# Twelve or fourteen combined block pairs in the down projection, with its casts and subtractions kept in program order

## The chip, the core and the metric

The kernel runs on one NeuronCore of a Trainium2 chip. The core has a matrix engine (TensorE, PE in the profile, with its weight loads shown apart as PEld), a vector engine (VectorE, DVE), a scalar engine (ScalarE, ACT), GpSimd (POOL) and SyncE (SP). In this kernel SP issues nearly all DMAs of weights and POOL issues a second, smaller stream. Matrix products accumulate in eight PSUM banks of 128 partitions by 512 float32 numbers.

The metric is the time of one execution on the device in microseconds (us), as the median of several runs. Lower is better.

## What is computed

One layer of a hybrid decoder: a combined input projection, eight heads of differential attention, four heads of chunked retention, an output projection with a residual, and then a gated MLP with a causal convolution. The last part is the one that matters here:

```python
def conv_glu(u, w_gate, w_up, conv_w, w_down):
    ...
    return (jax.nn.silu(gc) * (u @ w_up)) @ w_down
...
h = h + conv_glu(u, w_gate[l], w_up[l], conv_w[l], w_down[l])
out = rmsnorm(h, final_norm)
return out[:, CHUNK:]
```

Here D_MODEL is 2048, D_FF is 5632, and 256 positions are returned. The last product, the **down stage**, multiplies a 256 by 5632 matrix of activations by the 5632 by 2048 matrix `w_down`.

## The kernel before

**Three products for one.** All large products keep float32 accuracy with a faster reduced format. Each operand is split into a high part (a rounded copy) and a low part (the rest), and a product is a `triple` (lines 874 to 877) of three matmuls: high by high, high by low, low by high. For every weight tile of 128 partitions, ACT casts the raw float32 weights to the high part (`S.copy`, line 210), and DVE subtracts the high part from the raw weights to give the low part (line 211). This preparation of one entry is `prep(hf)`; the inner helper is `halves`. A cast and a subtraction go over 1024 columns in most cases.

**Stages.** The span runs through the input projection with attention and retention, the output projection, the gate and up projections (44 blocks `f` of 128 rows of D_FF, one gate and one up product each), and then the down stage, with nothing but small work after it.

**The down stage.** D_FF is cut in 44 blocks of 128. The output has 256 rows (two halves `m` of 128) and 2048 columns, worked in two *groups* `g` of 1024 columns (two halves `j` of 512 each). The blocks come in two kinds:

- `2*NS` blocks, here 24, are combined two by two into `NS` = 12 **pairs**. A pair is a 2 by 2 by 2 block product done with seven instead of eight products (a Strassen-Winograd scheme). It has four *parts* per group, each an entry that `prep` prepares: `d` with 1024 columns (two triples), `u` with 1024 columns (two triples), `t` with 1024 columns (two triples), `c` with 512 columns (one triple). After part `d` has been split, DVE also rewrites its 1024 raw columns in place as a difference (line 220), and part `t` is cast from that result.
- The remaining blocks, 20 before, are **plain**: `NPL` = 10 entries of two blocks for each 512-column half, called plain halves below. One has 1024 columns and four triples.

`down_order()` writes the order of entries: for each group some plain halves lead (`LEAD[g][0]`), then come the parts of all pairs with the remaining plain halves spread evenly between them, and some plain halves close the group (`LEAD[g][1]`). In the second group the last six (`HOLD`) are prepared but held back and multiplied at the very end.

**What sets the order of the work.** The program is written in order, and a scheduler at compile time fixes the order on each engine from its own estimate of when each instruction can run. An instruction wrapped in `keep` (`tc.keep_in_program_order`) stays in written order among the others so wrapped on its engine. `ahead(hf)` is called before each entry: it writes DMA loads for chunks that open up to six entries ahead and preparations up to three entries ahead. A prepared entry occupies one of four rings of high and low tiles (three `whi`/`wlo`, and `wx` for each fourth entry). Raw chunks rotate over five buffers (three `raw`, `sraw`, `act1`; the line with `turn`), so that the load of a chunk waits until the chunk five places before it has been read for the last time. A pair is one chunk and needs four DMAs, issued in this order on SP: its first half, the combined activations `sf`, the sums `td`, and `sw` for part `c` (lines 183 to 186). Plain chunks hold two plain halves, in one DMA of 1024 KB. `side` is a list of small tasks (joining the PSUM banks into the output, normalization), and `pump(n)` writes the next n of them.

**Sums for the pairs.** During the gate and up stage `stage()` has POOL load 768 KB of pair weights, `sums()` makes two DVE additions of 512 columns and has POOL write 512 KB back (`td`). There are two such sets for each pair. The activations of each pair are combined by DVE and ACT right after its second block (lines 835 to 847).

**Banks.** A group uses all eight PSUM banks: four for the direct outputs `(m, j)`, and four, named 1, 5, 6 and 7, for the combined products. `joined()` adds the latter into the output, `take(m, j)` adds a direct one.

Of the kernel before, what the change touches and what calls it, by code (L numbers as in the profile page):

```python
# [10 lines left out]
F32 = mybir.dt.float32  # L11
# [4 lines left out]
ALU = mybir.AluOpType  # L16
# [3 lines left out]
P = 128  # L20
# [20 lines left out]
NW = 512  # L41
# [3 lines left out]
LAM_INIT = 0.8 - 0.6 * math.exp(-0.3 * 0)  # L45
HK = KT // 2
HOLD = 6
NS = 12
KP = 2 * NS
NPL = (NF - KP) // 2  # L50
LEAD = [(4, 3), (2, HOLD + 2)]
PARTS = ("d", "u", "t", "c")
ROOMS = (0, 1, "2a", "2b", "3a", "3b")
FORMS = ("2a", "2b", "3a")
# [63 lines left out]
def trunk_kernel(ctx, tc, a, out):  # L118
    nc = tc.nc
    V, S, PE = nc.vector, nc.scalar, nc.tensor  # L120
# [74 lines left out]
    def prep(hf):  # L195
        c, s = entries[hf]
        held = len(entries) - 1 - hf
        if held < 2:
            hi, lo = [big.tile([P, 1024], F32R, tag=f"act{2 + held}{i}", name=f"end{held}{i}")
                      for i in "ab"]  # L200
        elif c >= nw and (hf - 2 * nw) % 4 == 3:
            wx = big.tile([P, 2 * 1024], F32R, tag="act0", name=f"wx{hf}")
            hi, lo = wx[:, :1024], wx[:, 1024:]
        else:
            hi = wp.tile([P, 1024], F32R, tag="whi", bufs=3, name=f"whi{hf}")
            lo = wp.tile([P, 1024], F32R, tag="wlo", bufs=3, name=f"wlo{hf}")

        def halves(src, b, e):
            with tc.high_priority() if 8 < hf < 16 else nullcontext():
                S.copy(out=hi[:, b:e], in_=src)  # L210
                V.tensor_tensor(out=lo[:, b:e], in0=src, in1=hi[:, b:e].bitcast(F32),  # L211
                                op=ALU.subtract)

        if c in mixed:
            g, p = divmod(mixed[c], NS)
            if s == "d":
                halves(raw[c][:, :2 * NW], 0, 2 * NW)
                two = raw[c][:, :2 * NW].rearrange("p (a c) -> p a c", a=2)
                t2 = raw[c][:, 2 * NW:3 * NW].unsqueeze(1).to_broadcast([P, 2, NW])
                V.tensor_tensor(out=two, in0=two, in1=t2, op=ALU.subtract)  # L220
            elif s == "u":
                halves(raw[c][:, 2 * NW:], 0, 2 * NW)
            elif s == "t":
                halves(raw[c][:, :2 * NW], 0, 2 * NW)
            else:
                halves(pools["sw"][g, p], 0, NW)
        else:
            halves(raw[c][:, s * 1024:(s + 1) * 1024], 0, 1024)
        pairs[hf] = (hi, lo)
        if s in (1, PARTS[-1]):  # L230
            raw.pop(c)
# [47 lines left out]
    def misc(name):  # L279
        return ps1.tile([P, 512], F32, tag="misc", bufs=3, name=name)  # L280
# [132 lines left out]
    def pump(n):  # L413
        for _ in range(n):
            if side:
                side.pop(0)()
# [351 lines left out]
    with ExitStack() as p2:  # L768
# [27 lines left out]
            stage()  # L796

        for f in range(NF):
            if f in (1, 2):
                stage()  # L800
            if staged and (f >= KP or f >= 4 and f % 2 == 0):
                sums()
            if f in (39, 41):
                m = (f - 39) // 2
                halfs.append(big.tile([P, D], F32, tag=f"htok{m}", name=f"htok{m}"))
                keep(nc.sync.dma_start(out=halfs[m], in_=hd[m * P:(m + 1) * P]))
            ps = gemm_q(idx, gs, 0)
            g = fw.tile([P, NQ], F32, tag="g", name=f"fg{f}")
            V.tensor_tensor(out=g, in0=ps[:, :NQ], in1=rstd2, op=ALU.mult)
            c = fw.tile([P, SEQ], F32, tag="c", name=f"fc{f}")  # L810
            V.tensor_scalar(out=c, in0=g[:, 0:SEQ], scalar1=cw[:, f, 0:1], scalar2=None,
                            op0=ALU.mult)
            for i in (1, 2):
                V.scalar_tensor_tensor(out=c, in0=g[:, i:i + SEQ], scalar=cw[:, f, i:i + 1],
                                       in1=c, op0=ALU.mult, op1=ALU.add)
            s = fw.tile([P, SEQ], F32, tag="s", name=f"fs{f}")
            S.activation(out=s, in_=c, func=AF.Silu)
            V.tensor_tensor(out=s, in0=s, in1=rstd2[:, 2:], op=ALU.mult)
            ps = gemm_t(idx + 1, gs)
            ul = fw.tile([P, SEQ], F32, tag="ul", name=f"ful{f}")  # L820
            S.copy(out=ul, in_=ps[:, SEQ:])
            u = ul
            V.tensor_tensor(out=u, in0=ps[:, :SEQ], in1=ul, op=ALU.add)
            V.tensor_tensor(out=u, in0=u, in1=s, op=ALU.mult)
            n = P if f < KP and f % 2 == 0 else SEQ
            S.copy(out=fhi[:, f, :n], in_=u[:, :n])
            V.tensor_tensor(out=flo[:, f, :n], in0=u[:, :n], in1=fhi[:, f, :n].bitcast(F32),
                            op=ALU.subtract)
            if f < KP and f % 2 == 0:
                us[f] = u  # L830
            elif f < KP:
                a1, a2 = us.pop(f - 1), u
                p = f // 2
                sm = fw.tile([P, 4, P], F32, tag="sm", bufs=1, name=f"sm{p}")
                V.tensor_tensor(out=sm[:, 0], in0=a1[:, P:], in1=a2[:, P:], op=ALU.add)
                V.tensor_tensor(out=sm[:, 1], in0=sm[:, 0], in1=a1[:, :P], op=ALU.subtract)
                V.tensor_tensor(out=sm[:, 2], in0=a1[:, :P], in1=a1[:, P:], op=ALU.subtract)
                V.tensor_tensor(out=sm[:, 3], in0=a2[:, :P], in1=sm[:, 1], op=ALU.subtract)
                s1 = fhi[:, f - 1, P:]
                S.copy(out=s1, in_=sm[:, 0])  # L840
                V.tensor_tensor(out=flo[:, f - 1, P:], in0=sm[:, 0], in1=s1.bitcast(F32),
                                op=ALU.subtract)
                sh = fw.tile([P, 2, 3, P], F32R, tag="sh", bufs=1, name=f"sh{p}")
                S.copy(out=sh[:, 0], in_=sm[:, 1:])
                V.tensor_tensor(out=sh[:, 1], in0=sm[:, 1:], in1=sh[:, 0].bitcast(F32),
                                op=ALU.subtract)
                keep(nc.gpsimd.dma_start(out=sd[p], in_=sh.rearrange("p a b c -> p (a b c)")
                                         .bitcast(F32)))
            idx += 2
# [79 lines left out]

        e = 2 * idx  # L930
        for g in range(2):
            mm = [ps1.tile([P, NW], F32, tag="mm", bufs=3, name=f"o{g}_{i}") for i in range(3)]
            bank = {(0, 0): mm[0], (0, 1): mm[1], (1, 0): mm[2], (1, 1): misc(f"o{g}_3")}
            bank[1], bank[6] = misc(f"x{g}_1"), misc(f"x{g}_6")
            xx = ps1.tile([P, 2, 512], F32, tag="sc", bufs=1, name=f"x{g}_57")
            bank[5], bank[7] = xx[:, 0], xx[:, 1]
            res = {(m, j): htok[:, m, (2 * g + j) * NW:(2 * g + j + 1) * NW]
                   for m in range(2) for j in range(2)}
            left = {1: NS, 5: NS, 6: NS, 7: NS}
# [2 lines left out]
                    left[m, j] = 2 * NPL + (NS if (m, j) != (1, 1) else 0)  # L942
            if g:
                left[1, 1] -= 2 * HOLD
            fresh = set(bank)

            def product(key, ac, wt, c0):
                left[key] -= 1
                ws = slice(c0, c0 + NW)
                triple(bank[key], *ac, wt[0][:, ws], wt[1][:, ws], key in fresh, left[key] == 0)  # L950
                fresh.discard(key)

            def joined():
                t = dn.tile([P, NW], F32, tag="t", name=f"t{g}")

                def f1():
# [23 lines left out]
            def weighed(m, n):  # L980
                return lambda: weigh(m, n * NW, (n + 1) * NW)

            def take(m, j):
                def f():
                    add(res[m, j], bank[m, j])
                return f
# [4 lines left out]
            for i, (kind, x, y) in enumerate(seq):  # L991
                ahead(e)
                if g and i >= len(seq) - HOLD:
                    held.append((y, e))
                    e += 1
                    continue
                wt = pairs[e]
                if kind == "w":
# [16 lines left out]
                if i == last_s:  # L1015
                    if g:
                        side.extend([weighed(m, n) for n in range(2) for m in range(2)])
                        side.append(lambda: norm(1))
                    side.extend(joined())
                    side.extend([take(0, 0), take(1, 0)])  # L1020
                    if g:
                        side.append(lambda: norm_scale(1))
                        for m in range(2):
                            side.extend([squared(m, 2), weighed(m, 2)])
                        side.append(lambda: S.activation(out=root, in_=so[:, 1, 2:3],
                                                         func=AF.Sqrt))
                pump(3 if i > last_s else 1)
            pump(len(side))
            if not g:
                take(0, 1)()  # L1030
                take(1, 1)()
                side.extend([nop] * 6)
                for m, n in ((0, 0), (1, 0), (0, 1), (1, 1)):
                    side.extend([squared(m, n), nop, nop])
                continue
            po = [bank[0, 1], bank[1, 1]]
            nb = NPL

# [19 lines left out]
            for c in range(2):  # L1058
# [2 lines left out]
                    down(o, 1, b, hf, c * HW, HW, start=i == 0, stop=i == HOLD - 1)  # L1061
                b_, e_ = LB + c * HW, LB + (c + 1) * HW
                hc = htok[:, 1, b_:e_]
                V.tensor_tensor(out=hc, in0=o, in1=hc, op=ALU.add)
                square(1, b_, e_, NB - 1 + c)
                weigh(1, b_, e_)
                if c == 0:
# [91 lines left out]
```

## Time and profile before

| | |
|---|---|
| median of 3 runs | 1150.26 us (1149.74 to 1150.60) |
| the profiled execution, its own time | 1150.52 us |
| its span from the first to the last instruction | 1148.4 us |
| PE busy | 1137.6 us (99% of the span) |
| DVE busy | 931.8 us (81%) |
| ACT busy | 605.7 us (53%) |
| mean granted TensorE clock | 0.999 of full speed |

The profiled execution's own time is 2.1 us longer than its span; that part lies before the first and after the last instruction. It is 0.26 us above the median of the runs. Busy time of PE overlaps with itself, since matmuls are pipelined, so 99% says that PE had work all the time, and the distance between the starts of two matmuls says how fast it went.

### The profile page before, as it was taken

What the parts mean: (1) busy time and instruction counts of PE and PEld (TensorE: products, weight loads), DVE (VectorE), ACT (ScalarE), POOL (GpSimd) and SP (SyncE); (2) the same over time, 40 slices, a digit from 0 to 9 for tenths busy, and PEclk for the clock granted to TensorE, in tenths of its full rate; (3) what the DMA queues carried; (4) which work ended last, traced back from release to release, by engine and by line L of the source; (5) the groups of instructions that cost most, each with busy time, mean ns of one, the idle gap of its engine ahead of it and who ended that gap; (6) DMA issues with size and microseconds to landing.
All of it is one profiled execution on the core that took longest, in us unless ns stands there. A gap on an engine that the chain in (4) does not pass through costs nothing.

```text
span 1148.4 us, 20659 instructions
## 1 busy us (share of the span) xinstructions
PE 1137.6 (99%) x7967; PEld 1066.1 (93%) x7967; DVE 931.8 (81%) x1738; ACT 605.7 (53%) x997; POOL 36.4 (3%) x84
## 2 busy tenths in 40 slices
PE   8999999999999999999999999999999999999997
PEld 7999999999999999999999999999999988888886
DVE  7898787667677769888888888888877778898897
ACT  7676665443345545444445444444444456556663
POOL 0000000000000000000000000100000000000000
PEclk9999999999999999999999999999999999999999
DMA  9644546565648775766776777888876588877872
GB/s 314 215 156 160 183 140 196 166 224 165 208 157 251 236 230 190 286 244 256 280 255 246 275 286 267 297 310 303 318 261 223 196 335 302 291 285 247 312 279 92
DMA packets 96018, 276.76 MB, mean 241 GB/s; under 512 B 43856, under 2 KB 52176, under 8 KB 74160
## 3 DMA queue, kind: packets, MB, share of 16 engines
q1 hardware_dynamic: 87616, 238.08, 59.7%
q0 software_dynamic: 8160, 37.23, 8.6%
q8 instruction: 62, 1.02, 0.3%
q14 instruction: 36, 0.29, 0.1%
q10 hardware_dynamic: 144, 0.14, 0.1%
HBM read 251.56 MB, written 23.86 MB: 240 GB/s over the span
## 4 chain that ended last, share of the span: by engine, by line
PE 98%; ACT 1%; DMA 0%; DVE 0%; SPq 0%; issue 0%; DVEq 0%; ACTq 0%
PE mm L463 14%; PE mm L452 10%; PE mm L450 10%; PE mm L451 10%; PE mm L442 7%; PE mm L443 7%; PE mm L444 7%; PE mm L465 7%; PE o L876 4%; PE o L877 4%; PE o L875 4%; PE x L875 2%; PE x L877 2%; PE x L876 2%; PE po L587 1%; PE ro L642 1%
## 5 line engine op out<-in xcount | busy, mean ns | idle before, releaser
L210 ACT CAST whi<-raw 128x1024 fp32r<-128x1024 f32 x379 | 397.9, 1052 | 376.6 <-issue 92.1
L211 DVE TENSOR_TENSOR wlo<-raw,whi 128x1024 fp32r<-128x1024 f32 x379 | 462.6, 1223 | 132.5 <-ACT whi L210 125.6
L463 PE MATMUL mm<-g,whi 128*128 128x512 f32 x352 | 124.4, 392 | 0.0
L452 PE MATMUL mm<-g,wlo 128*128 128x258 f32 x352 | 99.4, 282 | 0.0
L442 PE MATMUL mm<-x,whi 128*128 128x272 f32 (+1 forms) x344 | 99.3, 289 | 0.0
L450 PE MATMUL mm<-g,whi 128*128 128x260 f32 x352 | 99.2, 282 | 0.0
L444 PE MATMUL mm<-x,wlo 128*128 128x272 f32 (+1 forms) x344 | 99.0, 288 | 0.0
L443 PE MATMUL mm<-x,whi 128*128 128x272 f32 (+1 forms) x344 | 98.9, 287 | 0.0
L465 PE MATMUL mm<-g,wlo 128*128 128x256 f32 x352 | 98.6, 280 | 0.0
L451 PE MATMUL mm<-g,whi 128*128 128x256 f32 x352 | 97.8, 278 | 0.0
L463 PEld LDWEIGHTS mm<-g,whi 128*128 128x128 f32 x352 | 66.1, 188 | 13.1
L450 PE MATMUL mm<-ys,whi 128*128 128x260 f32 x256 | 71.9, 282 | 0.0
L452 PE MATMUL mm<-ys,wlo 128*128 128x258 f32 x256 | 71.8, 281 | 0.0
L451 PE MATMUL mm<-ys,whi 128*128 128x256 f32 x256 | 70.7, 276 | 0.0
L451 PEld LDWEIGHTS mm<-g,whi 128*128 128x128 f32 x352 | 66.7, 189 | 1.9
L465 PEld LDWEIGHTS mm<-g,wlo 128*128 128x128 f32 x352 | 66.2, 188 | 0.0
L450 PEld LDWEIGHTS mm<-g,whi 128*128 128x128 f32 x352 | 66.1, 188 | 0.0
L452 PEld LDWEIGHTS mm<-g,wlo 128*128 128x128 f32 x352 | 66.0, 188 | 0.0
L443 PEld LDWEIGHTS mm<-x,whi 128*128 128x128 f32 x344 | 64.9, 189 | 0.0
L444 PEld LDWEIGHTS mm<-x,wlo 128*128 128x128 f32 x344 | 64.8, 188 | 0.0
L442 PEld LDWEIGHTS mm<-x,whi 128*128 128x128 f32 x344 | 64.8, 188 | 0.0
L876 PE MATMUL o<-wlo,fhi 128*128 128x512 f32 x149 | 58.1, 390 | 0.0
(404 smaller groups left out, 3061.6 us busy)
## 6 DMA issues: line engine op xcount, KB each, us to landing
raw<-in_w_in_dram SPq DMA_DIRECT2D x44, 1024.0 KB, 4.9
raw<-in_w_gate_dram SPq DMA_DIRECT2D x44, 1024.0 KB, 5.2
raw<-in_w_up_dram SPq DMA_DIRECT2D x44, 1024.0 KB, 5.3
raw<-in_w_down_dram SPq DMA_DIRECT2D x20, 1024.0 KB, 6.7
ts<-in_w_mix_dram POOLq DMA_DIRECT2D x24, 768.0 KB, 5.1
raw<-in_w_out_dram SPq DMA_DIRECT2D x16, 1024.0 KB, 5.2
td<-ts POOLq DMA_DIRECT2D x24, 512.0 KB, 5.3
raw<-in_w_mix_dram SPq DMA_DIRECT2D x24, 512.0 KB, 6.5
```

The lines of the kernel that those rows point to most:

```text
L210: S.copy(out=hi[:, b:e], in_=src)
L211: V.tensor_tensor(out=lo[:, b:e], in0=src, in1=hi[:, b:e].bitcast(F32), op=ALU.subtract)
L442: PE.matmul(ps[:, :n], wh, xh, start=(k == 0), stop=False)
L443: PE.matmul(ps[:, :n], wh, xl, start=False, stop=False)
L444: PE.matmul(ps[:, :n], wl, xh, start=False, stop=(k == KT - 1))
L450: PE.matmul(ps[:, :NQ + 2], wh, src.cols(k, GO - 2, GL), start=(k == 0), stop=False)
L451: PE.matmul(ps[:, 4:NQ + 2], wh, src.cols(k, GL, GW), start=False, stop=False)
L452: PE.matmul(ps[:, 2:NQ + 2], wl, src.hi(k), start=False, stop=(k == KT - 1))
L463: PE.matmul(ps, wh, src.cols(k, GO + 2, GW), start=(k == 0), stop=(k == KT - 1))
L465: PE.matmul(ps[:, :SEQ], wl, src.cols(k, GO + 2, GL), start=False, stop=False)
L875: PE.matmul(o, ah, wh, start=start, stop=False)
L876: PE.matmul(o, ah, wl, start=False, stop=False)
```

## The change

Pairs go from 12 to 14, so that 28 of the 44 blocks are combined and 16 are plain (eight plain halves for each 512-column half). The lead and tail of the two groups become 4 and 6, and 4 and 8. From the fifth entry of the down stage on, casts, subtractions and the in-place difference are wrapped in `keep`. The sums in the gate and up stage run in three of four blocks from the third block on. PSUM tiles of the down stage are allocated at their first use. At the end of the first group the joining tasks are pumped one per plain half instead of three, the last two additions move into the second group, and in the second group two tasks are pumped for each held half.

```diff
-NS = 12
+NS = 14
-LEAD = [(4, 3), (2, HOLD + 2)]
+LEAD = [(4, 6), (4, HOLD + 2)]
...
+        pin = keep if hf >= 2 * nw + 4 else (lambda ins: ins)
+
         def halves(src, b, e):
             with tc.high_priority() if 8 < hf < 16 else nullcontext():
-                S.copy(out=hi[:, b:e], in_=src)
-                V.tensor_tensor(out=lo[:, b:e], in0=src, in1=hi[:, b:e].bitcast(F32),
-                                op=ALU.subtract)
+                pin(S.copy(out=hi[:, b:e], in_=src))
+                pin(V.tensor_tensor(out=lo[:, b:e], in0=src, in1=hi[:, b:e].bitcast(F32),
+                                    op=ALU.subtract))
...
-                V.tensor_tensor(out=two, in0=two, in1=t2, op=ALU.subtract)
+                pin(V.tensor_tensor(out=two, in0=two, in1=t2, op=ALU.subtract))
...
-            if f in (1, 2):
+            if f < 2:
                 stage()
-            if staged and (f >= KP or f >= 4 and f % 2 == 0):
+            elif staged and f % 4 != 3:
                 sums()
-            if f in (39, 41):
-                m = (f - 39) // 2
+            if f in (41, 42):
+                m = f - 41
...
-            mm = [ps1.tile([P, NW], F32, tag="mm", bufs=3, name=f"o{g}_{i}") for i in range(3)]
-            bank = {(0, 0): mm[0], (0, 1): mm[1], (1, 0): mm[2], (1, 1): misc(f"o{g}_3")}
-            bank[1], bank[6] = misc(f"x{g}_1"), misc(f"x{g}_6")
...
+            def room(key):
+                if key in bank:
+                    return bank[key]
+                if key in (5, 7):
+                    xx = ps1.tile([P, 2, 512], F32, tag="sc", bufs=1, name=f"x{g}_57")
+                    bank[5], bank[7] = xx[:, 0], xx[:, 1]
+                elif key in ((0, 0), (1, 0), (0, 1)):
+                    bank[key] = ps1.tile([P, NW], F32, tag="mm", bufs=3,
+                                         name=f"o{g}_{key[0]}{key[1]}")
+                else:
+                    bank[key] = misc(f"o{g}_11" if key == (1, 1) else f"x{g}_{key}")
+                return bank[key]
...
                 if g and i >= len(seq) - HOLD:
                     held.append((y, e))
                     e += 1
+                    pump(2)
                     continue
...
-                    side.extend(joined())
-                    side.extend([take(0, 0), take(1, 0)])
+                    side.extend([take(0, 0), take(1, 0), *joined()])
...
-                pump(3 if i > last_s else 1)
-            pump(len(side))
+                pump(3 if g and i > last_s else 1)
             if not g:
-                take(0, 1)()
-                take(1, 1)()
-                side.extend([nop] * 6)
+                side.extend([take(0, 1), take(1, 1)] + [nop] * 6)
...
                 continue
+            pump(len(side))
...
-                V.tensor_tensor(out=hc, in0=o, in1=hc, op=ALU.add)
+                keep(V.tensor_tensor(out=hc, in0=o, in1=hc, op=ALU.add))
```

More of the change, by code (lines that the diff above doesn't have):

```diff
@@ L931, in trunk_kernel @@
         for g in range(2):
-            mm = [ps1.tile([P, NW], F32, tag="mm", bufs=3, name=f"o{g}_{i}") for i in range(3)]
-            bank = {(0, 0): mm[0], (0, 1): mm[1], (1, 0): mm[2], (1, 1): misc(f"o{g}_3")}
-            bank[1], bank[6] = misc(f"x{g}_1"), misc(f"x{g}_6")
-            xx = ps1.tile([P, 2, 512], F32, tag="sc", bufs=1, name=f"x{g}_57")
-            bank[5], bank[7] = xx[:, 0], xx[:, 1]
+            bank = {}
+            def room(key):
[10 more added lines that the diff above has]
+                return bank[key]
             res = {(m, j): htok[:, m, (2 * g + j) * NW:(2 * g + j + 1) * NW]
@@ L944, in trunk_kernel @@
                 left[1, 1] -= 2 * HOLD
-            fresh = set(bank)
+            fresh = set(left)
             def product(key, ac, wt, c0):
@@ L949, in product, with joined @@
                 ws = slice(c0, c0 + NW)
-                triple(bank[key], *ac, wt[0][:, ws], wt[1][:, ws], key in fresh, left[key] == 0)
+                triple(room(key), *ac, wt[0][:, ws], wt[1][:, ws], key in fresh, left[key] == 0)
                 fresh.discard(key)
-            def joined():
+            def joined(bank=bank, res=res):
                 t = dn.tile([P, NW], F32, tag="t", name=f"t{g}")
@@ L981, in weighed, with take @@
                 return lambda: weigh(m, n * NW, (n + 1) * NW)
-            def take(m, j):
+            def take(m, j, bank=bank, res=res):
                 def f():
```

## The prediction

> **What bounds the kernel now.** I read the page's span and its chain first, then the busy table by stretches, then the waits of PE's weight loads.
>
> ```profile
> span 1148.4 us, 20659 instructions
> PE 98%; ACT 1%; DMA 0%; DVE 0%; SPq 0%; issue 0%; DVEq 0%; ACTq 0%
> ```
> ```profile
> core 0: us, PE busy (x) PEld busy (x) DVE busy (x) ACT busy (x) POOL busy (x), PEclk, DMA share, GB/s
> 457.00:707.00 250.00, 250.00 (x1786) 235.09 (x1785) 207.12 (x379) 122.26 (x202) 18.52 (x35) 1.00 0.71 265
> 707.00:860.00 153.00, 153.00 (x1087) 143.53 (x1086) 127.19 (x203) 69.60 (x109) 13.14 (x25) 1.00 0.83 301
> 916.00:1030.00 114.00, 114.00 (x506) 94.42 (x505) 97.76 (x99) 67.77 (x76) 0.54 (x1) 1.00 0.87 314
> 1030.00:1115.00 85.00, 85.00 (x376) 70.19 (x375) 75.35 (x71) 54.73 (x63) 0.00 (x0) 1.00 0.76 271
> 1115.00:1136.00 21.00, 21.00 (x110) 17.97 (x109) 20.96 (x30) 10.49 (x14) 0.54 (x1) 1.00 0.21 76
> ```
> ```profile
> PEld x L875 <- ACT wx L210: 0.3, 1, 0.3
> ```
>
> 98% of the chain is PE. The first two rows are gate and up, the next two the groups of the down stage, the last its tail. PE is never idle in them, at clock 1.00. The last fence is all that PE's weight loads waited from 457 us on: once, 0.3 us. So the time is the number of matmuls times their spacing. But DVE is already busy 75.35 of 85 us in the second group and 20.96 of 21 in the tail.
>
> **What goes.** A group now has 12x7 + 20x4 = 164 triples, afterwards 14x7 + 16x4 = 162. Two groups, three matmuls each: 12 matmuls of 512 columns less.
>
> ```profile
> 1050.17 0.39 PE L876 MATMUL o<-wlo,fhi 128*128 128x512 f32 x1
> ...
> 1052.89 0.39 PE L875 MATMUL o<-whi,fhi 128*128 128x512 f32 x1
> ```
>
> From the first to the last of these 13 matmuls there are 12 steps and 2.72 us, 0.227 us each. The gain is thus 12 x 0.227 = **2.72 us**; I find nothing that could make it larger.
>
> **What comes, in the down stage.** A group has four entries more (72 for 68). Two more pairs bring six 1024-column and two 512-column preparations and two in-place differences; four plain halves take four preparations away. Over both groups DVE gets 4 subtractions of 1024 columns, 4 of 512 and 4 differences.
>
> ```profile
> 1080.34 1.22 DVE L211 TENSOR_TENSOR wlo<-raw,whi 128x1024 fp32r<-128x1024 f32 x1
> 1081.47 1.22 DVE L220 TENSOR_TENSOR raw<-raw 128x1024 f32<-128x1024 f32 x1
> 1082.61 1.22 DVE L211 TENSOR_TENSOR wlo<-raw,whi 128x1024 fp32r<-128x1024 f32 x1
> 1083.74 0.68 DVE L211 TENSOR_TENSOR wx<-b,wx 128x512 fp32r<-128x512 f32 x1
> 1084.35 1.22 DVE L211 TENSOR_TENSOR wlo<-raw,whi 128x1024 fp32r<-128x1024 f32 x1
> ```
>
> Starts are 1.13 to 1.14 us apart after 1024 columns (I take 1.135) and 0.61 after 512, so DVE gets 4x1.135 + 4x0.61 + 4x1.135 = 11.5 us more while PE gets 2.7 less. It now decides whether the gain is kept. Per pair DVE needs 4x1.135 + 0.61 = 5.15 us, PE 21x0.227 = 4.76: a pair costs 0.38 us of DVE's lead. A plain half gives back 12x0.227 - 1.135 = 1.59. Before, a plain half followed each four or five parts. The written order afterwards (W a plain half):
>
> ```
> group 1: WWWW dutcdutcdu W tcdutcdut W cdutcdutc W dutcdutcd W utcdutcdu W tcdutcdutc WWWWWWW
> group 2: WWWW dutcdutcdutcdu W tcdutcdutcdutc W dutcdutcdutcdu W tcdutcdutcdutc WWWWWWWWW
> ```
>
> Part by part DVE needs 2.27, 1.135, 1.135, 0.61 us for d, u, t, c and PE 1.36, 1.36, 1.36, 0.68. The runs between plain halves cost 1.44, 0.54, 0.69, 1.67, 0.54, 0.46 in the first group and 1.83, 0.84, 1.83, 0.84 in the second.
>
> Against that stands the lead that DVE can hold. With four rings an entry's cast starts when the entry four before it is done; the three parts between (t, u and c) last PE 3.4 us; cast and subtraction take 1.05 + 1.22 plus 0.14 of signals by the rows of the next part (0.11 from DVE to ACT, 0.03 from ACT to DVE): lead **1.0 us**. PE adds to it, since only the middle matmul of a triple reads the low part:
>
> ```profile
> 1091.20 0.39 PE L875 MATMUL x<-whi,fhi 128*128 128x512 f32 x1
> 1091.44 0.50 PE L875 MATMUL x<-wx,fhi 128*128 128x512 f32 x1
> 1091.78 0.40 PE L876 MATMUL o<-wlo,fhi 128*128 128x512 f32 x1
> ```
>
> Here two high products of coming parts were put ahead, 2x0.227 = 0.45: lead **1.45**. A run that costs more than the lead stalls PE by the rest; the next plain half refills it, up to the limit. With 1.0: 0.44 + 0.67 in the first group, 2x0.83 in the second, 2.8 us. With 1.45: 0.22 + 2x0.38 = 1.0.
>
> **The pinned order** adds a wait. Part t can only be cast after the difference, and with d, difference, u, t, c pinned DVE has just u in between.
>
> ```profile
> 1109.89 1.22 DVE L220 TENSOR_TENSOR raw<-raw 128x1024 f32<-128x1024 f32 x1
> 1112.30 1.23 DVE L211 TENSOR_TENSOR wlo<-raw,whi 128x1024 fp32r<-128x1024 f32 x1 [1.20 <-ACT whi L210]
> ```
> ```profile
> 1111.22 1.05 ACT L210 CAST whi<-raw 128x1024 fp32r<-128x1024 f32 x1 [2.50 <-DVE raw L220]
> ```
>
> From the start of the difference to t's subtraction at least 2.41 us pass; difference and u fill 2.27. So 0.14 us a pair where DVE has no lead; where the free order put t next, as here, 1.20 were lost, so pinning gains too. Behind the waiting subtraction stand c and the next d; behind t's cast on ACT, c's and d's casts. If each pair pays 0.14, the stalls become 5.0 (lead 1.0) or 2.4 (lead 1.45). The longer lead is nearer to the rows, since before's order, reckoned alike (two runs d, u, t, c, d of 1.29), should have waited 0.6 with 1.0 and nothing with 1.45, and waited 0.3. The 0.14 is paid in the later half of a run: between 1.0 and 2.4 I take **1.7 us**, and keep 0 and 5.0 as ends.
>
> **Transfers.** Four DMAs of a pair move 1664 KB.
>
> ```profile
> L183 SPq DMA_DIRECT2D raw<-in_w_mix_dram x24: 328/426/536, 910.7 to 1093.0; - x24
> ...
> DMA to landing us min/median/max: 3.6/6.5/9.7
> ```
> ```profile
> raw<-in_w_down_dram SPq DMA_DIRECT2D x20, 1024.0 KB, 6.7
> raw<-td SPq DMA_DIRECT2D x24, 512.0 KB, 7.7
> ```
>
> 14 pairs per 77.5 us of mixed PE time in the second group (14x4.76 + 4x2.72) and four plain halves of 512 KB are 25.3 MB, 327 GB/s, against 314 in the row for 916 to 1030 at 0.87 of DMA's time. That fits, tightly. What is new is the rotation of five raw buffers: a plain chunk keeps its buffer for both of its halves, and these are now up to 14 parts apart. In the second group the ninth pair takes the buffer of the chunk whose later half is the second W between parts. Its load goes out only after that subtraction, 5.15 us of DVE before it is wanted, 4.1 before its cast. A landing after 3.6 us costs nothing, one after 6.5 some 2.5 us. SP's queue has then stood empty for over 5 us behind this load, so I take the short landing: nothing. Twice more the distance is short: the twelfth pair of the first group (6.9 us), and the last W chunk but two, two halves after its predecessor, where PE has 8.2 us and a 6.7 us landing, cast and subtraction take 9.1: 0 to 0.9, taken as nothing. What the blocked load holds up on SP, the next pairs, has two pairs of time.
>
> **Edits at nothing.** In gate and up, two more pairs and four more sums:
>
> ```profile
> L793 DVE TENSOR_TENSOR ts<-ts 128x512 f32<-128x512 f32 x24 | 16.5, 688 | 0.5
> L845 DVE TENSOR_TENSOR sh<-sm,sh 128x384 fp32r<-128x384 f32 x12 | 6.6, 549 | 0.0
> L835 DVE TENSOR_TENSOR sm<-ful,ful 128x128 f32<-128x128 f32 x11 | 3.2, 293 | 0.4
> ```
> ```profile
> 439.49 0.23 PE mm L463
> ...
> 911.57 0.23 PE mm L463
> ```
>
> A sum is 2x0.69 us; a pair 0.55 and five such as the last row, 2.0 together. The second fence is the first and the last of 43 such steps of the chain, one a block: PE takes 472.08/42 = 11.24 us a block, and DVE is busy 207.12/250 of that, 9.3. An odd block that gets both, new with this change, reaches at most 9.3 + 1.0 + 0.7 = 11.0: covered, by 0.2 us; uncovered it would cost tenths in six blocks, within 0 to 2 us. POOL is at 18.52 of 250. ACT's casts, 4x1.05 us and 4 of half the columns more, lie in its 54.73 of 85. Banks allocated at first use lift no wait that PE has. The joins at the change of group are:
>
> ```profile
> 1121.00 0.68 DVE L928 TENSOR_TENSOR htok<-x,htok 128x512 f32<-128x512 f32 x1
> 1121.60 0.68 DVE L928 TENSOR_TENSOR t<-x,t 128x512 f32<-128x512 f32 x1
> ```
>
> 0.60 us each, twelve of them: 7.2 us beside ten plain halves, which take PE 27.2 us and DVE 11.4. They are hidden, as they were before; if they delayed the second group's first pair, they would cost the 1.0 us of lead. In the tail the work is the same and slack remains:
>
> ```profile
> 1136.42 0.42 DVE L1064 TENSOR_TENSOR htok<-oe,htok 128x256 f32<-128x256 f32 x1 [0.41 <-PE oe L877]
> ...
> 1140.73 0.42 DVE L1064 TENSOR_TENSOR htok<-oe,htok 128x256 f32<-128x256 f32 x1 [1.16 <-PE oe L877]
> ```
>
> DVE waited 0.41 and 1.16 us for PE there; an arrival up to 1 us later is covered, more isn't.
>
> **Sum.** 1150.52 - 2.72 + 1.7 = 1149.5 for the profiled execution, which stands 0.26 above the median: **1149.2 us**.
>
> **Rivals.**
> - *No stall.* The compile-time order moves more low products back than the two shown, and the lead covers the runs. Then 1150.26 - 2.72 = 1147.5. For it: the single 0.3 us wait before. Against it: runs three times as long.
> - *Slower: the held raw buffer.* The mechanism sits at the ninth pair of the second group. If its load lands after the median 6.5 us, DVE stands 2.5 us with nothing in its lead; the two other short distances add 0.7 and 0.9, and without lead the runs cost 2.8: 6.9 - 2.72 = +4.2, 1154.4. It decides once landings at a blocked buffer exceed 4.1 us, and the kernel is measurably slower when all stalls pass 5.0 us. The 5.0 of pinned order and short lead lies at that border too.
> - *DVE pays whole durations.* If in a full queue an operation started only when the one before had ended, a pair would take 4x1.22 + 0.69 = 5.57 us of DVE, 0.81 beyond PE, and a plain half would give back 1.50. The runs would cost 2.6, 1.5, 1.6, 2.7, 1.5, 1.5 and 3.4, 2.3, 3.4, 2.3; less 1.0 of lead each they stall PE 12.8 us: 1160.3. The rows above speak against it, starts 1.14 apart for operations of 1.22. The Trainium skill says so in "VectorE: DVE Perf Modes", section Terms: DVE flushes its pipeline after every operation, and the next can't issue until the pipe is empty. The trace disagrees with that, by the starts just named.
> - *Doesn't do what it says.* If the scheduler orders PE for another DVE than the real one, pinning changes nothing and PE stalls in front of each t; that falls in the same two cases by its size.
>
> **How the numbers follow.** A measurement can tell about 0.2% (2.3 us) from no change. The forecast, stalls of 0.4 to 5.0 us, 1147.96 to 1152.56, has 0.45. No stall, under 0.4, has 0.32: the bound is reached by a lead only some 0.4 us longer than I took. The slower cases have 0.23: 0.21 the held buffer or the 5.0 of pinned order, 0.02 the whole durations. The range goes from 1147.4, the full gain, to 1153.6, most of the way to the slower rival.
>
> **What would show it.** PE's weight loads wait for DVE's low parts, mostly in the second group on t and u just before a W; total 1 to 2.5 us. Down-stage matmuls fall by 12 and DVE's busy share in the second group rises above 95%. The transfer rival would show as ACT casts waiting for DMA at the ninth pair. It is wrong if gate and up stretches past 11.24 us a block, or if the tail after the last matmul grows.

## The result and the profile after

| | before | after |
|---|---|---|
| median of 6 runs each | 1150.22 us (1149.74 to 1150.60) | 1159.17 us (1158.76 to 1159.39) |
| span of the profiled execution | 1148.4 us | 1157.3 us |
| start of the last matmul | 1140.41 us | 1144.75 us |
| from there to the end of the span | 8.0 us | 12.55 us |

The changed kernel is 0.8% **slower**, ratio 1.0077 with a 95% interval of 1.0065 to 1.0090; 1149.2 us were predicted. Below are the busy line of the page of after, then one stretch of each group of the down stage in its table by stretches (PE, weight loads, DVE, ACT and POOL in us, then clock, DMA share, GB/s), then the second of these stretches in before:

```profile
PE 1140.0 (99%) x7955; PEld 1062.8 (92%) x7955; DVE 949.8 (82%) x1770; ACT 612.8 (53%) x1009; POOL 41.6 (4%) x94
```
```profile
936.00:1016.00 80.00, 79.00 (x340) 63.01 (x339) 76.44 (x74) 52.65 (x58) 0.00 (x0) 1.00 0.89 315
1046.00:1116.00 70.00, 68.97 (x295) 54.27 (x293) 67.62 (x64) 46.66 (x52) 0.00 (x0) 1.00 0.89 322
```
```profile
1046.00:1116.00 70.00, 70.00 (x310) 57.76 (x309) 62.71 (x59) 45.02 (x49) 0.00 (x0) 1.00 0.83 300
```

PE still counts as busy 99% of the time in after, but it starts only 295 matmuls in the 70 us of the second row, 4.2 per us. Before started 310, which is the 1 / 0.227 = 4.4 per us of the spacing. DVE is busy 96.6% there, before 89.6%. The busy share of PE hides lost time: a matmul is listed with 0.39 us and the next one starts 0.227 us after it, so a start that comes up to 0.16 us late leaves no idle time, and a later one leaves less than it lost. The waits of PE's weight loads show it (from 400 us on: waited for, us in total, times, longest):

```profile
PEld o L877 <- ACT whi L212: 4.9, 9, 0.8
PEld o L877 <- ACT wx L212: 2.2, 4, 0.8
PEld x L878 <- DVE wlo L213: 2.0, 3, 0.7
PEld x L878 <- DVE wx L213: 0.3, 1, 0.3
PEld o L878 <- DVE wlo L213: 0.2, 1, 0.2
```

9.6 us in all where before had 0.3, and 7.1 of them not for a low part of DVE but for a *cast* of ACT. The down stage starts at 916.51 us (before 916.63). So the 8.9 us that the span grew are: 0.12 less ahead of the down stage, 2.72 less for the twelve matmuls, 7.2 of stalls (the last matmul starts at 1144.75, and without stalls it would at 1140.41 - 0.12 - 2.72 = 1137.57), and 12.55 - 8.0 = 4.55 behind the last matmul.

**One pair.** DVE's timeline in the second group of after (start, duration, instruction):

```profile
1067.86 1.23 DVE L222 TENSOR_TENSOR raw<-raw 128x1024 f32<-128x1024 f32 x1
1069.00 1.22 DVE L213 TENSOR_TENSOR wlo<-raw,whi 128x1024 fp32r<-128x1024 f32 x1
1070.28 1.23 DVE L213 TENSOR_TENSOR wx<-raw,wx 128x1024 fp32r<-128x1024 f32 x1
1071.42 0.68 DVE L213 TENSOR_TENSOR wlo<-b,whi 128x512 fp32r<-128x512 f32 x1
1072.02 1.22 DVE L213 TENSOR_TENSOR wlo<-raw,whi 128x1024 fp32r<-128x1024 f32 x1
1073.28 1.23 DVE L222 TENSOR_TENSOR raw<-raw 128x1024 f32<-128x1024 f32 x1
1074.42 1.22 DVE L213 TENSOR_TENSOR wlo<-raw,whi 128x1024 fp32r<-128x1024 f32 x1
```

From difference to difference (L222) 5.42 us pass. Two of the steps are longer than the usual 1.135: u to t, 1.28, because t's cast waits for the difference; and d's subtraction to the difference, 1073.28 - 1072.02 = 1.26, because the difference overwrites what that subtraction reads and starts when it has ended. On ACT and PE of after the next t looks like this:

```profile
1074.61 1.05 ACT L212 CAST wx<-raw 128x1024 fp32r<-128x1024 f32 x1 [1.79 <-DVE raw L222]
```
```profile
1074.97 0.39 PE L879 MATMUL o<-whi,sf 128*128 128x512 f32 x1
1075.71 0.50 PE L877 MATMUL o<-wx,fhi 128*128 128x512 f32 x1 [0.36 <-ACT wx L212]
1076.05 0.40 PE L878 MATMUL x<-wlo,sf 128*128 128x512 f32 x1
```

The cast starts 0.1 us after the difference has ended (1073.28 + 1.23) and ends at 1075.66. PE's order has t's high product (L877) next and then u's low product (third line). The former starts 0.74 us after its predecessor, not 0.227: 0.51 us lost, in one pair. The name behind the wait, a cast of ACT, doesn't mean that ACT is slow: it had stood idle for 1.79 us. Nor would another order have helped PE here: u's subtraction, the last DVE row, ends at 1075.64 too. DVE is late, and both things that PE could do next hang on it.

**The end.** DVE's timeline of after, the last held halves and the sums that follow them:

```profile
1135.06 1.22 DVE L213 TENSOR_TENSOR end1b<-raw,end1a 128x1024 fp32r<-128x1024 f32 x1
...
1137.46 1.22 DVE L213 TENSOR_TENSOR end0b<-raw,end0a 128x1024 fp32r<-128x1024 f32 x1
...
1143.87 0.69 DVE L1055 TENSOR_TENSOR htok<-o,htok 128x512 f32<-128x512 f32 x1 [3.93 <-PE o L879]
...
1147.78 0.42 DVE L1074 TENSOR_TENSOR htok<-oe,htok 128x256 f32<-128x256 f32 x1
...
1149.37 0.41 DVE L1074 TENSOR_TENSOR htok<-oe,htok 128x256 f32<-128x256 f32 x1
...
1151.58 1.15 DVE L1086 TENSOR_SCALAR htok<-htok,fz 128x256 f32<-128x256 f32 x3
```

and the same of before:

```profile
1123.33 1.22 DVE L211 TENSOR_TENSOR end1b<-raw,end1a 128x1024 fp32r<-128x1024 f32 x1
1124.47 1.22 DVE L211 TENSOR_TENSOR end0b<-raw,end0a 128x1024 fp32r<-128x1024 f32 x1
...
1135.33 0.68 DVE L1045 TENSOR_TENSOR htok<-o,htok 128x512 f32<-128x512 f32 x1
...
1142.95 1.15 DVE L1076 TENSOR_SCALAR htok<-htok,fz 128x256 f32<-128x256 f32 x3
```

Before, the last two subtractions started 17 and 16 us before PE's last matmul, and PE's last product of the upper row half (`o`) started 6.5 us before the lower one's (`oe`), so the upper half's normalization ran beside PE. After, they start 9.7 and 7.3 us ahead, PE's last products of the two halves start 1.3 us apart, and the two normalizations run one behind the other with PE already done.

PE's timeline of before, the last product of each half, and then that of after:

```profile
1133.96 0.39 PE L877 MATMUL o<-end0a,flo 128*128 128x512 f32 x1
...
1140.41 0.28 PE L877 MATMUL oe<-end0a,flo 128*128 128x256 f32 x1
```
```profile
1143.44 0.39 PE L879 MATMUL o<-end0a,flo 128*128 128x512 f32 x1
...
1144.75 0.28 PE L879 MATMUL oe<-end0a,flo 128*128 128x256 f32 x1
```

### The profile page after: what moved, and what is told of

It is laid out like the page before. It is cut to its first block, busy times and chain, and to the rows that moved or that the text cites. A ratio compares the mean times of both kernels' runs of the same rounds, so it can differ in the third digit from the quotient of the medians.

```text
span 1157.3 us, 20735 instructions
## 1 busy us (share of the span) xinstructions
PE 1140.0 (99%) x7955; PEld 1062.8 (92%) x7955; DVE 949.8 (82%) x1770; ACT 612.8 (53%) x1009; POOL 41.6 (4%) x94
## 4 chain that ended last, share of the span: by engine, by line
PE 90%; DVE 4%; ACT 2%; issue 2%; DMA 1%; SPq 0%; DVEq 0%; ACTq 0%
PE mm L465 14%; PE mm L454 10%; PE mm L452 10%; PE mm L453 10%; PE mm L444 7%; PE mm L445 7%; PE mm L446 7%; PE mm L467 7%; PE o L877 3%; PE o L878 3%; PE o L879 3%; DVE wlo L213 2%; DVE raw L222 1%; ACT whi L212 1%; PE x L878 1%
## 5 line engine op out<-in xcount | busy, mean ns | idle before, releaser
L823 ACT COPY ful<-mm 128x256 f32<-128x256 f32 x44 | 16.4, 373 | 78.2 <-PE mm L465 75.7
```

## The experiments

Theory 1: with 14 pairs DVE paces the pairs (5.42 us against PE's 4.76), and the end is late by the order of the last subtractions. Theory 2: pinning itself costs the time, by waits at the head of a queue. All edits are to the kernel after. "Stalls" is the start of the last matmul less 1137.57 (less 1140.29 with 12 pairs); "end" is the span from that start on. The first matmul of the down stage starts between 915.92 and 916.72 us in these runs, and the column of stalls doesn't allow for that, so differences of up to some 0.6 us in it mean nothing; a stall below zero is none. Each ratio is to runs of before that were measured together with that run.

| run | median us | ratio to before (95%) | last matmul | stalls | end | weight loads waited |
|---|---|---|---|---|---|---|
| before | 1150.2 | | 1140.41 | | 8.0 | 0.3 |
| after | 1159.17 | 1.0077 (1.0065 to 1.0090) | 1144.75 | 7.2 | 12.55 | 9.6 |
| e1_no_pin | 1165.66 | 1.0133 (1.0118 to 1.0148) | 1153.80 | 16.2 | 9.7 | 20.9 |
| e2_tail_free | 1156.27 | 1.0050 (1.0033 to 1.0067) | 1144.85 | 7.3 | 9.75 | 9.7 |
| e3_twelve | 1155.63 | 1.0045 (1.0030 to 1.0060) | 1141.32 | 1.0 | 12.5 | 1.5 |
| e4_spread | 1156.09 | 1.0050 (1.0035 to 1.0065) | 1141.45 | 3.9 | 12.65 | 5.7 |
| e5_no_diff | 1152.39 | 1.0019 (1.0009 to 1.0028) | 1137.54 | 0.0 | 12.55 | 0.9 |
| e6_aside | 1154.48 | 1.0040 (1.0025 to 1.0055) | 1139.86 | 2.3 | 12.6 | 3.9 |
| e7_pool | 1198.19 | 1.0418 (1.0402 to 1.0433) | 1183.1 | 45.5 | 12.5 | 43.7 |
| e8_spread_tail | 1153.38 | 1.0026 (1.0015 to 1.0036) | 1141.51 | 3.9 | 9.7 | 5.8 |
| e9_duct | 1156.12 | 1.0050 (1.0032 to 1.0068) | 1141.84 | 4.3 | 12.6 | 6.1 |
| e10_all | 1150.99 | 1.0006 (0.9997 to 1.0016) | 1139.46 | 1.9 | 9.75 | 3.5 |
| e11_hc | 1150.67 | 1.0002 (0.9993 to 1.0012) | 1139.45 | 1.9 | 9.15 | 3.3 |
| e12_pins12 | 1152.20 | 1.0016 (1.0006 to 1.0025) | 1140.02 | -0.3 | 10.1 | 0.3 |
| e13_wider | 1155.10 | 1.0045 (1.0031 to 1.0059) | 1142.83 | 5.3 | 9.9 | 7.9 |
| e14_twelve_all | 1150.81 | 1.0003 (0.9994 to 1.0012) | 1139.71 | -0.6 | 9.0 | 0.0 |

**No pinning at all.**

```diff
-        pin = keep if hf >= 2 * nw + 4 else (lambda ins: ins)
+        pin = lambda ins: ins
```

> The changed kernel with no cast, subtraction or difference pinned. Its loss against the 1147.5 us of an undisturbed run has two parts in its trace: 7.2 us in which PE stalls between the pairs, and 4.5 us more between the last matmul and the end. Theory 1 (spacing: VectorE needs 5.42 us for a pair where PE needs 4.76, and the plain halves are too far apart): most of the 7.2 stays, 4 to 6 us of it, while the end gets 3 to 4 us shorter, since the low parts of the held halves come earlier: 1152 to 1155. Theory 2 (the pins alone stall PE): both parts go, 1147.5 to 1149. Theory 3 (pinning helps in the pairs, the loss is all in the end): the pairs get worse, the end better: 1155 to 1158.

The span is 6.2 us longer than after's: 9.05 us more of stalls and 2.85 us less at the end. In DVE's timeline the free order puts t straight behind the difference, where its cast can't be ready:

```profile
1093.28 1.22 DVE L222 TENSOR_TENSOR raw<-raw 128x1024 f32<-128x1024 f32 x1
1095.68 1.23 DVE L213 TENSOR_TENSOR wlo<-raw,whi 128x1024 fp32r<-128x1024 f32 x1 [1.19 <-ACT whi L212]
```

1.19 us of DVE lost, and DVE has none to spare. Theory 2 falls for the pairs: pinning gains there. For the end it is right, which the next run takes by itself. The run as a whole went the way of the expectation's third theory, pairs worse and end better, but 1165.66 us lies far beyond its 1155 to 1158; and theory 1, that most of the stalls stay and none are added, missed too.

**Pins off for the last nine entries alone.**

```diff
-        pin = keep if hf >= 2 * nw + 4 else (lambda ins: ins)
+        pin = keep if 2 * nw + 4 <= hf < len(entries) - 9 else (lambda ins: ins)
```

> The changed kernel, with the last nine entries (the plain halves behind the last pair of the second group) unpinned, all else pinned. Theory of the end (pinned subtractions of the held halves stand behind the joining additions, so that the last products of the upper row half end together with those of the lower one): the end between last matmul and last instruction falls from 12.3 to about 8 us, the pairs stay as they are: 1154.5 to 1155.5. If the pins in the end don't matter: 1159.

The stalls stay and the end falls from 12.55 to 9.75 us: 2.8 of the 4.55 us come from the pins on these nine entries, six of which are the held halves. The rest does not, and the expected 8 us are missed; in this run the upper half's sum (L1055) still comes at 1141.10, 3.75 us before the last matmul, where before had 5.1.

**Twelve pairs, everything else of the change kept.**

```diff
-NS = 14
+NS = 12
```

> The changed kernel with 12 pairs instead of 14, all else as changed (pins, leads 4 and 6, 4 and 8, one joining task beside each half). Theory 1 (spacing): runs of at most six parts stall PE little, under 2 us, and the end keeps its 4 to 5 us: 1154 to 1157. Theory 2 (pins alone): stalls of 6 us like those of the changed kernel stay, with the end's: 1159 to 1161.

The stalls fall to 1.0 us, the end stays. So most of the stalls come with the two pairs and the longer runs that they make, and the end has nothing to do with them.

**The plain halves spread more.** Shorter lead and tail leave more plain halves between the parts of pairs, so that the runs of parts are shorter.

```diff
-LEAD = [(4, 6), (4, HOLD + 2)]
+LEAD = [(4, 3), (2, HOLD + 2)]
```

> The changed kernel with the leads and tails of the kernel before (4 and 3, 2 and 8): nine plain halves between the parts of the first group for six, six for four in the second. Theory 1 (spacing): the runs are five to ten parts long instead of nine to fourteen, PE's 7.2 us of stalls fall to 2 to 4, and the change of group costs under 1 us: 1153.5 to 1156. Theory 2 (pins alone): 1159 as changed. A loss at the change of group, with its fewer plain halves, would show as new PE waits there and give 1158 or more.

Stalls 7.2 to 3.9 us: over two fifths of them come from the length of the runs, with the same pairs.

**The difference left out, and the difference without its dependences.** In the second, DVE does the same operation at the same place, but writes to a tile that nothing reads. In both, part t is cast from the raw columns as they came, so the difference is missing from what they compute.

```diff
-                pin(V.tensor_tensor(out=two, in0=two, in1=t2, op=ALU.subtract))
```
```diff
-                pin(V.tensor_tensor(out=two, in0=two, in1=t2, op=ALU.subtract))
+                aside = pools["dn"].tile([P, 2 * NW], BF16, tag="aside", name=f"as{hf}")
+                pin(V.tensor_tensor(out=aside.rearrange("p (a c) -> p a c", a=2), in0=two,
+                                    in1=t2, op=ALU.subtract))
```

> The changed kernel without the in-place difference of each pair, which is left out of the computation; part t is cast from the raw columns as they came. VectorE then needs 4.0 us for a pair where PE needs 4.76. Theory 1 (VectorE's 5.42 us for a pair make PE's 7.1 us of stalls): the stalls fall under 0.5 us, PE's last matmul comes at about 1138 us, the end keeps its 12.5: 1152 to 1152.8. If late transfers or ACT's casts make the stalls: 3 us or more stay, 1155 or more.

> The changed kernel with the difference written to a buffer that nobody reads (as bfloat16, for want of room), so that VectorE does the same work but part t's cast waits for nothing; part t's values are those of the raw columns, so the output isn't the reference's. A pair then takes VectorE 5.15 us instead of 5.42, without the 0.14 us for t's cast and the 0.12 us between the subtraction and the rewriting in place. If those two small waits carry the error of my sum: stalls 1 to 3 us, 1153 to 1155.5. If the work alone makes the stalls: 1157.5 to 1159.

Without the operation nearly all stalls go. From the first to the last matmul of the down stage 221.46 us pass (916.08 to 1137.54), in before 223.78 (916.63 to 1140.41): 2.32 of the 2.72 us are gained, and the weight loads still wait 0.9 us. That the last matmul starts so near to 1137.57 is in part luck, since this down stage began 0.43 us earlier than that of after. With the operation but without its dependences 2.3 us of stalls remain of 7.2. DVE's timeline of that run:

```profile
1063.56 1.22 DVE L213 TENSOR_TENSOR wlo<-raw,whi 128x1024 fp32r<-128x1024 f32 x1
1064.70 1.22 DVE L223 TENSOR_TENSOR as<-raw 128x1024 bf16<-128x1024 f32 x1
1065.83 1.22 DVE L213 TENSOR_TENSOR wlo<-raw,whi 128x1024 fp32r<-128x1024 f32 x1
1066.97 1.22 DVE L213 TENSOR_TENSOR wx<-raw,wx 128x1024 fp32r<-128x1024 f32 x1
1068.10 0.69 DVE L213 TENSOR_TENSOR wlo<-b,whi 128x512 fp32r<-128x512 f32 x1
1068.70 1.23 DVE L213 TENSOR_TENSOR wlo<-raw,whi 128x1024 fp32r<-128x1024 f32 x1
```

Now the first step is 1.14, not 1.26, and a pair takes 1068.70 - 1063.56 = 5.14 us: the prediction's 5.15. So the two waits, 0.12 + 0.14 us in each of the 28 pairs (14 a group), are what 4.9 us of the stalls come from. They don't add up one to one, which would be 28 x 0.26 = 7.3 us, since what falls into the lead costs nothing.

**The difference on GpSimd.** It would take 1.14 us a pair off DVE.

```diff
-                pin(V.tensor_tensor(out=two, in0=two, in1=t2, op=ALU.subtract))
+                pin(nc.gpsimd.tensor_tensor(out=two, in0=two, in1=t2, op=ALU.subtract))
```

> The changed kernel with the difference made by GpSimd in place of VectorE. VectorE is relieved to 4.0 us a pair, but part t waits for GpSimd, whose time for such an operation no run has shown yet. If it takes up to 2.2 us: stalls under 2 us, 1152 to 1154. If it takes over 3.5 us or slows VectorE down: 1157 to 1165.

A miss by far. The first fence is GpSimd's group, the others one stretch of the two engines' timelines:

```profile
L222 POOL TENSOR_TENSOR raw<-raw 128x1024 f32<-128x1024 f32 x28 | 83.5, 2983 | 149.2 <-DVE wlo L213 122.8 <-DVE wx L213 26.3
```
```profile
945.12 2.41 POOL L222 TENSOR_TENSOR raw<-raw 128x1024 f32<-128x1024 f32 x1 [4.16 <-DVE wlo L213]
951.75 3.25 POOL L222 TENSOR_TENSOR raw<-raw 128x1024 f32<-128x1024 f32 x1 [4.22 <-DVE wlo L213]
```
```profile
945.79 2.82 DVE L213 TENSOR_TENSOR wlo<-raw,whi 128x1024 fp32r<-128x1024 f32 x1 [0.75 <-ACT whi L212]
```

The operation takes 2.98 us on average where DVE takes 1.23, and t's cast waits for all of it. Beside that a DVE subtraction that starts within it takes 2.82 us; it ends at 948.61, 1.08 after the other one's end (945.12 + 2.41), as if it had begun only then. The Trainium skill, page "SBUF — State Buffer", section "Who interferes with whom", says this: a Vector instruction with two inputs in SBUF contends with a GpSimd instruction that reads SBUF, the ports that they share are an exclusive lock, and the order of issue decides which of the two is blocked. The trace agrees, by these rows.

**Spread and free end together.**

```diff
-LEAD = [(4, 6), (4, HOLD + 2)]
+LEAD = [(4, 3), (2, HOLD + 2)]
...
-        pin = keep if hf >= 2 * nw + 4 else (lambda ins: ins)
+        pin = keep if 2 * nw + 4 <= hf < len(entries) - 9 else (lambda ins: ins)
```

> Fourteen pairs with the leads and tails of the kernel before, and the last nine entries unpinned: the two edits that each took 3 us from the changed kernel. If the losses add up as the traces say (3.2 us in the pairs, 2.9 at the end): 1153.0 to 1153.6. If the end takes back what the pairs give: 1155 or more.

Stalls 3.9 and end 9.7: the two gains add up, so they are two causes.

**Part c ahead of part t.** This gives the difference and its cast 0.61 us more before t's subtraction is due.

```diff
-PARTS = ("d", "u", "t", "c")
+PARTS = ("d", "u", "c", "t")
```

> The changed kernel with the parts of each pair in the order d, u, c, t instead of d, u, t, c, so that VectorE has two subtractions between the difference and t's. That takes away the 0.14 us a pair for t's cast and leaves the 0.12 for the rewriting in place: 5.27 us a pair. By runs of parts the stalls fall from 7.1 to about 4 us: 1155.5 to 1157. If the order of parts doesn't matter: 1159. If the cast of t were what holds PE in each pair: 1153 to 1154.5.

DVE's timeline has the wait at t gone and the one at the difference left:

```profile
1065.92 1.23 DVE L222 TENSOR_TENSOR raw<-raw 128x1024 f32<-128x1024 f32 x1
1067.06 1.22 DVE L213 TENSOR_TENSOR wlo<-raw,whi 128x1024 fp32r<-128x1024 f32 x1
1068.19 0.69 DVE L213 TENSOR_TENSOR wx<-b,wx 128x512 fp32r<-128x512 f32 x1
1068.80 2.35 DVE L213 TENSOR_TENSOR wlo<-raw,whi 128x1024 fp32r<-128x1024 f32 x2
1071.19 1.23 DVE L222 TENSOR_TENSOR raw<-raw 128x1024 f32<-128x1024 f32 x1
```

5.27 us a pair, stalls 7.2 to 4.3.

**All three, and then the last addition not kept.** The first run has the edits of e8_spread_tail and e9_duct; the second has this one besides:

```diff
-                keep(V.tensor_tensor(out=hc, in0=o, in1=hc, op=ALU.add))
+                V.tensor_tensor(out=hc, in0=o, in1=hc, op=ALU.add)
```

> Fourteen pairs, leads and tails of the kernel before, the last nine entries unpinned, and parts in the order d, u, c, t. From the 1153.4 of the first two together, 1 to 2 us of the 3.9 that PE still stalls go: 1151.4 to 1152.4. If the three overlap: 1153.

> The kernel of the run before it, with the addition of the lower row half's last columns not pinned either, as before the change. In the orders on VectorE this addition then stands ahead of the upper half's scaling instead of behind it. If that place makes the 1.7 us by which the end is still longer than before (9.7 for 8.0): 1.5 to 1.8 us less than that run, 1150 to 1150.8. If the lateness of the subtractions makes it: no change.

The first comes out a little better than expected, at 1150.99 us. The second lands in the expected range, but the step to it is a miss: DVE's last scaling (L1086) starts 1.17 us earlier, at 1142.25 for 1143.42, but the span falls only 0.6 and the median 0.3. Behind the last scaling 6.35 us pass there and 5.45 in before. In that run the upper half's output transfers go out at 1140.75 and 1141.2, shortly before the last ones; that the two groups of transfers hinder each other is a guess that no run tested. This version is level with before (1.0002), and none of the runs is faster than before.

**The pins alone, with twelve pairs.**

```diff
-NS = 14
+NS = 12
-LEAD = [(4, 6), (4, HOLD + 2)]
+LEAD = [(4, 3), (2, HOLD + 2)]
...
-        pin = keep if hf >= 2 * nw + 4 else (lambda ins: ins)
+        pin = keep if 2 * nw + 4 <= hf < len(entries) - 9 else (lambda ins: ins)
```

> Twelve pairs with the leads and tails of the kernel before and pins up to the last nine entries: pinning by itself, without more pairs. If pinning costs nothing where plain halves stand every four or five parts: PE's last matmul as before at 1140.4, the end 9.7 us because of the pinned addition of the last columns: 1151.7 to 1152.3. If pinning by itself stalls PE by 0.14 to 0.26 us a pair: 1155 or more.

With a plain half behind every three to five parts the pinned order costs PE nothing: one wait of 0.3 us, as before. The end is still 2.1 us longer than before's, with stalls and pinned held halves both gone.

**Still fewer parts in a row**, on e11_hc, with only the LEAD line different:

```diff
-LEAD = [(4, 3), (2, HOLD + 2)]
+LEAD = [(2, 3), (2, HOLD + 1)]
```

> The kernel of run e11 with leads and tails 2 and 3, 2 and 7: eleven plain halves between the parts of the first group for nine, seven for six in the second. Of e11's 1.9 us of PE stalls, spacing would leave 0.5 to 1.5, so 1149.3 to 1150.4 with the end as in e11. If those stalls have another cause than the spacing, or the shorter tail makes the end later: 1150.7 or more.

A miss: stalls 5.3 us, not fewer. The weight loads wait 3.3 us in the first pairs, at 915 to 935 us, where ACT waits for DMA up to 2.4 us. Another 4.6 us of waits come in the second group, and about 2 us of the stalls are left for them. From 1000 to 1130 us ACT's largest wait is for PE:

```profile
ACT whi L212 <- PE o L879: 23.1, 17, 2.3
```

These 17 casts waited up to 2.3 us for PE to be done with the tile that they overwrite. That doesn't single out the cause: from 1040 to 1112 us the same wait comes to 12.7 us here and to 10.6 us in e11_hc, which stalls less. What holds PE in the second group of this run stays open.

**The same order with twelve pairs**, the edits of e11_hc and `NS = 12`:

> The kernel of run e11 with 12 pairs: VectorE has 11.5 us less to do there. If the end (9.1 us after the last matmul in e11, 8.0 before the change) is late because VectorE comes late out of the pairs: the end falls to about 8.2, PE's last matmul at 1140.1: 1150.0 to 1150.4. If the end is late through the order of the tail alone: 9.1 stays, 1151 to 1151.5. With 14 pairs faster than these by 0.5 us or more, the pairs would earn something; otherwise their 2.72 us are spent.

The weight loads wait for nothing at all, and the time is that of e11_hc: 1150.81 and 1150.67 us. From the first to the last matmul of the down stage 223.50 us pass with twelve pairs and 223.10 with fourteen. So of the 2.72 us that two more pairs take out of PE's work, 0.4 are left even in the best order found. The end of 9.0 us is there without them, so it isn't late because DVE comes late out of the pairs; the time stayed under the 1151 us expected for that case because the last matmul started 0.4 us earlier than expected.

## Why the prediction was wrong

**What held.** The twelve matmuls are worth 2.72 us: e5_no_diff gains 2.32 of them, with 0.9 us of waits left. Gate and up didn't stretch: the down stage begins 0.12 us earlier, so the edits at nothing there cost nothing. DVE became the bound, at 95.6 and 96.6% busy in the two stretches, as the signs had it. The held raw buffer cost DVE nothing: at the ninth pair of the second group u's cast waited 0.79 us for its transfer, and u's subtraction still came 1.15 us after the difference. ACT's waits for raw tiles of DMA from 400 us on are five, of 1.1 us at most. The sum of the transfers took a KB as 1000 bytes; with the profile's 1024 it asks for 335 GB/s and not 327, and 322 were moved in the second row of the result.

**The failing step: the price of a pair.** The prediction put 5.15 us of DVE on a pair, and counted the 0.14 us of t's cast half, as paid only in the later part of a run. It is 5.42. The 0.14 is paid wherever DVE has no lead, and that is most of the long runs. The other 0.12, between d's subtraction and the difference that overwrites its input, wasn't in the working at all, though the trace of before shows it:

```profile
1043.79 1.23 DVE L211 TENSOR_TENSOR wx<-raw,wx 128x1024 fp32r<-128x1024 f32 x1 [0.73 <-ACT wx L210]
1045.05 1.22 DVE L220 TENSOR_TENSOR raw<-raw 128x1024 f32<-128x1024 f32 x1
1046.19 1.22 DVE L211 TENSOR_TENSOR wlo<-raw,whi 128x1024 fp32r<-128x1024 f32 x1
```

1.26 us to the difference, 1.14 behind it. The row from which the prediction took the step, 1080.34 to 1081.47, has a plain half's subtraction ahead of the difference, since the free order had put it between; the pinned order never does. Reckoned with the prediction's own method, a pair takes 0.66 us of lead instead of 0.38, the runs cost 2.1, 1.2, 1.3, 2.4, 1.1, 1.2 and 2.8, 1.8, 2.8, 1.8, and what goes beyond the lead is 5.0 us with a lead of 1.45 and 8.5 with 1.0. 7.2 was measured, between the two, against 1.7 predicted with an upper end of 5.0. So the term that was mis-sized is the stalls, through the unit price: off by 5%, it moved the result fourfold, because the stalls are what is left of the runs after the lead, a small difference of larger numbers. Reckoned alike, the two leads also enclose what e4_spread (1.6 to 5.4), e6_aside (0.8 to 2.6) and e9_duct (2.4 to 4.7) measured. They fail for e13_wider, where they give 0.2 to 1.4 and 5.3 came, so the length of the runs isn't all that counts.

**Where PE waits** was half right. The prediction had it wait for low parts and counted high products as work that PE can put ahead. 7.1 of the 9.6 us are waits for casts, all thirteen of them for t's: this cast can't start before the difference is done, so t's high product, which was counted as work that can go ahead, comes no sooner than u's low part. And 4.1 of the 9.6 us lie in the first group, where the second was to have most of them.

**The end.** "In the tail the work is the same and slack remains" was priced at nothing; it cost 4.55 us. The work is the same, but the pins and the joining tasks put ahead of the held halves' subtractions moved these by 11.7 and 13.0 us, of which the stalls ahead of them explain at most 7.2, and PE's order of the two row halves changed with them. 2.8 us go when the last nine entries are not pinned. Of the other 1.75 the runs show only that they don't depend on the number of pairs (9.15 with 14, 9.0 with 12, in the same order) and that the last addition, when it is not kept in order, gives back 0.6; how the rest divides between the joining tasks, PE's order and the output transfers stays open. The prediction's range had no term for this at all, though it named a longer tail as a sign that it was wrong. The two errors together close the account: 1149.2 + (7.2 - 1.7) + 4.55 - 0.12 = 1159.1 us, and 1159.17 came.

**The rivals.** That DVE pays whole durations, held at 0.02, gave 1160.3, and 1159.17 came. It is still wrong: independent operations start 1.13 to 1.14 us apart in after too (1069.00 after 1067.86). Only an operation that depends on the one before waits its whole 1.22, one in five of a pair. It named 12.8 us of stalls and 7.2 came; the 4.55 us at the end, which it didn't have, made up most of the difference, so its nearness is luck. The slower rival of the raw buffer did not happen; "doesn't do what it says" neither, as e1_no_pin shows: pinning saves 9 us of stalls. Pinning, that the prediction named as a cost and a gain, is needed for fourteen pairs and harmful at the end.

## What to carry to other kernels

Where an edit takes work from the bounding engine and gives it to one that is nearly full, read the second engine's price from the very sequence it will run, dependences between neighbours included, and not from the same instructions in another order; 0.26 us in 5.4 made 4.9 of the 7.2 us of stalls here. Look at the stretch with the longest run without relief, not at the mean, and ask what the error of the unit price does to what remains beyond the lead. An order that is pinned for the steady part should end where the drain begins, which was worth 2.8 us here: there the question is no longer throughput but which result is finished first.

## What the runs showed of the hardware

- An fp32 DVE operation of 128x1024 takes 1.22 us and the next independent one starts after 1.135; one that overwrites what the operation before it reads starts after 1.26 (before and after alike). The same operation with another destination, of bf16, starts after 1.14 (e6_aside).
- The same operation on GpSimd takes 2.38 to 3.48 us, and a DVE subtraction that started within one took 2.82 us instead of 1.22; with 28 of them the kernel is 39 us slower than after (e7_pool).
